# The delta rule's key and query lengths: squares in feature layout, summed by TensorE with a column of ones, in place of transposes and statistics

## The chip, the cores and the metric

The kernel runs on one core of one Trainium2 chip. The metric is the device time of one execution in microseconds (us). The engines are TensorE (PE, with its weight loads listed as PEld), VectorE (DVE), ScalarE (ACT), GpSimd (POOL) and the queue of SyncE (SP), which starts most loads of weights.

## The reference, cut to what matters

One inference step of a four-layer decoder: 256 new rows of a prompt (one sequence) and 8 single rows of samples, 1024 features. The mixers are pooling, gated delta rule, retention, pooling; each is followed by a SwiGLU block. The change is in the delta rule (layer 1), where queries and keys of each of 8 heads are divided by their lengths over 128 features:

```python
def l2norm(x):
    return x * lax.rsqrt(jnp.sum(x * x, -1, keepdims=True) + RMS_EPS)
...
    q = l2norm(qkv[..., :H * dk].reshape(B, T, H, dk)) * dk ** -0.5
    k = l2norm(qkv[..., H * dk:2 * H * dk].reshape(B, T, H, dk))
    v = qkv[..., 2 * H * dk:].reshape(B, T, H, dv)
    beta = jax.nn.sigmoid(b_logit)
    ...
    o, S = gated_delta_rule(q, k, v, g, beta, S0.astype(F32))
```

The delta rule then solves, for each head and chunk, a triangular system made of the products of keys with keys, and multiplies its result with values, queries and a running state.

## The kernel before, in words

All activations lie with features on the 128 partitions and the 264 rows (T: 256 prompt rows, then 8 sample rows) along the free axis. Weights come in chunks of 128 x 2048 and are split into a high and a low part (ScalarE casts at L205 and L231, VectorE or GpSimd subtracts at L206 and L232), so a projection is three fast matmuls for each block (`mm3`, all of them on L123, the line of the matmul helper; transposes are on L128).

The delta-rule layer (`gdn_layer`) takes heads in four pairs. It has 16 projections, two heads each, in the order of the list `jobs`: four of keys, one gate, then queries, values and gates mixed. After a projection come a short convolution (VectorE, L651 and L654) and SiLU (ScalarE, L657); the keys of all pairs stand in `kt` (128 x 8 x 264), queries in tiles of the tag `qv0`.

`lengths` gives the reciprocal lengths of one pair with rows on partitions, as `ssq` (128 x 2 heads x 3 columns: two chunks of 128 prompt rows and one of the 8 samples). Because lengths are sums over partitions in the feature layout, it transposes: four transposes of 128 x 128 into one PSUM tile `pk`, two of the sample columns into `pks`. For the heads in `onv` VectorE takes bn_stats and bn_aggr (mean and variance, from which the sum of squares is made); for the others ScalarE squares and sums (L802). GpSimd raises to the power -1/2 (L810, L811). `ON_V` says that both heads of key pairs 0 and 1, and the second head of pairs 2 and 3, go to VectorE; queries go to ScalarE.

Small PSUM tiles (`sm_ps`, tag `sm`) share four buffers; those of projections (`mm`) have four others. SBUF tiles of one tag share `bufs` buffers, one where none is given.

Most instructions are ordered by a scheduler that simulates the engines and starts what is ready, in the order of the program where there is a choice. From `PE.pinned = True` on, each TensorE instruction is kept behind the TensorE instruction written before it. There the work is woven by hand: `weave(main, fill, ratio)` runs one piece of `main` and then `ratio` steps of `fill` on average, a step being one block (`mm3`, three matmuls) of a projection; a piece ends at each `yield`. `turns` goes round several generators, `seq` runs them one after the other. Before that point the key lengths of pairs 0 to 2 are made, then the gate's projection, then the lengths of pair 3. The first woven part is `inverse` for all pairs (it begins with `br`, the key lengths times beta, on GpSimd at L819, then transposes of `br` and products of keys with keys, L825 and L831 on VectorE); the next are `operands`, `sample` and `outputs` for pairs 0 and 1, then for 2 and 3. The query lengths are the last thing in `operands`, after the products of keys with queries (L926); they are needed at the end of `outputs`.

Of the kernel before, what the change touches and what calls it, by code (L numbers as in the profile page):

```python
# [11 lines left out]
F32 = mybir.dt.float32  # L12
F32R = mybir.dt.float32r
BF16 = mybir.dt.bfloat16
AF = mybir.ActivationFunctionType
ALU = mybir.AluOpType
ADD, SUB, MUL, MAX, MIN, POW = ALU.add, ALU.subtract, ALU.mult, ALU.max, ALU.min, ALU.pow
AX = mybir.AxisListType

P = 128  # L20
TP = 256
NB = 8
T = TP + NB
# [6 lines left out]
RMS_EPS = 1e-6  # L30
DK = 128
# [9 lines left out]
RATIO = (0.8, 2, 1)  # L41

LO_FROM, LO_PARTS = 5, (0, 1, 3)
ON_V = ((0, 1), (0, 1), (1,), (1,))
ON_G = (3, 5, 7)
ATANH = (1.0000000039388743, 0.3333315796753999, 0.2001242686175498, 0.13980709417099926, 0.14087328632969365)

# [64 lines left out]
def body(ctx: ExitStack, tc: tile.TileContext, ap):  # L112
    nc = tc.nc
    V, S, G = nc.vector, nc.scalar, nc.gpsimd
# [29 lines left out]
    def C(name):  # L144
        o, n = CL[name]
        return cst[:, o:o + n]
# [5 lines left out]
    ident, U, sl, ones, o1024 = (C(n) for n in ("ident", "u", "sl", "ones", "o1024"))  # L152
    mhalf = pers.tile([P, 24], F32, name="mhalf")
# [34 lines left out]
    def nm(s):  # L188
        uid[0] += 1
        return f"{s}_{uid[0]}"  # L190
# [6 lines left out]
    def sm_ps(shape):  # L197
        return psm.tile(shape, F32, tag="sm", name=nm("sm"))
# [422 lines left out]
    def gdn_layer(l, pln):  # L621
        gp = ctx2.enter_context(tc.tile_pool(name="gdn", bufs=1))
# [36 lines left out]
        kt = gp.tile([P, H, T], F32, name="kt")  # L659
# [31 lines left out]
        for t in range(3):  # L691
            n = P if t < 2 else NB
# [76 lines left out]
        rks, rqs, brs, kgs, kbs, vbs, ats, tts, oss, oos = ({} for _ in range(10))  # L769

        def tile4(tag, bufs=1, dt=F32):
            return gp.tile([P, 2, 2, P], dt, tag=tag, name=nm(tag), bufs=bufs)

        def ct(tag, bufs=2):
            return gp.tile([P, 2, 3], F32, tag=tag, name=nm(tag), bufs=bufs)

        def hsl(a, p):
            return a[:, :, 2 * p:2 * p + 2].rearrange("p t h -> p h t")

        def lengths(src, tag, onv=()):  # L780

            pk, pks = sm_ps([P, 2, 2, P]), sm_ps([P, 2, P])
            ssq = ct(tag, 4)
            V.memset(ssq[:, :, 2], 1.0)
            if onv:
                mv = gp.tile([P, 2, 3, 2], F32, tag="mv", name=nm("mv"), bufs=2)
                V.memset(mv[:, :, 2], 1.0)
            for h in range(2):
                for c in range(2):
                    PE.transpose(pk[:, h, c], src[h][:, c * P:(c + 1) * P], ident)  # L790
            for h in range(2):
                PE.transpose(pks[:NB, h], src[h][:, TP:T], ident)
            for h in range(2):
                jk = gp.tile([P, P], F32, tag="junk", name=nm("junk"))
                for c in range(3):
                    n, a = (P, pk[:, h, c]) if c < 2 else (NB, pks[:NB, h])
                    if h in onv:
                        bs = gp.tile([P, 6], F32, tag="bs", name=nm("bs"), bufs=2)
                        V.bn_stats(bs[:n], a)
                        V.bn_aggr(mv[:n, h, c], bs[:n])  # L800
                    else:
                        S.activation(jk[:n], a, AF.Square, accum_out=ssq[:n, h, c:c + 1])  # L802
                if h in onv:
                    sh = ssq[:, h]
                    V.tensor_tensor(sh, mv[:, h, :, 0], mv[:, h, :, 0], MUL)
                    V.tensor_tensor(sh, sh, mv[:, h, :, 1], ADD)
                    V.tensor_scalar(sh, sh, float(DK), None, MUL)
            V.tensor_scalar(ssq, ssq, RMS_EPS, None, ADD)
            mh = mhalf[:, 0:6].rearrange("p (a b) -> p a b", a=2)
            G.tensor_tensor(ssq[:, :, 0:2], ssq[:, :, 0:2], mh[:, :, 0:2], POW)  # L810
            G.tensor_tensor(ssq[:NB, :, 2], ssq[:NB, :, 2], mh[:NB, :, 2], POW)  # L811
            return ssq

        def inverse(p):
# [84 lines left out]
        def operands(p):  # L899

            h0 = 2 * p
            q, v, rk, br = qt[p], vt[p], rks[p], brs[p]
            skg, skb = ct("skg"), ct("skb")
            G.tensor_tensor(skg[:, :, 0:2], rk[:, :, 0:2], hsl(egk, p)[:, :, 0:2], MUL)
            G.tensor_tensor(skb[:, :, 0:2], br[:, :, 0:2], hsl(egc, p)[:, :, 0:2], MUL)
            pk = sm_ps([P, 2, 2, P])
            for h, c in hc:
                PE.transpose(pk[:, h, c], kt[:, h0 + h, c * P:(c + 1) * P], ident)
            kg = kgs[p] = tile4("t1", 4)
            kb = kbs[p] = lnp.tile([P, 2, P], F32, tag="sq", name=nm("kb1"), bufs=2)  # L910
            V.tensor_tensor(kg, pk, skg[:, :, 0:2].unsqueeze(3).to_broadcast([P, 2, 2, P]), MUL)
            for h in range(2):
                S.mul(kb[:, h], pk[:, h, 1], skb[:, h, 1:2])
            yield
            pv = sm_ps([P, 2, 2, P])
            for h, c in hc:
                PE.transpose(pv[:, h, c], v[:, h, c * P:(c + 1) * P], ident)
            vb = vbs[p] = tile4("t1", 4)
            V.tensor_tensor(vb, pv, hsl(beta, p)[:, :, 0:2].unsqueeze(3).to_broadcast([P, 2, 2, P]), MUL)
            yield  # L920
            at = ats[p] = tile4("t2", 4)
            pqk = sm_ps([P, 2, 2, P])
            for h, c in hc:
                PE.matmul(pqk[:, h, c], kt[:, h0 + h, c * P:(c + 1) * P], q[:, h, c * P:(c + 1) * P], start=True, stop=True)
            for h, c in hc:
                V.scalar_tensor_tensor(at[:, h, c], pqk[:, h, c], rk[:, h, c:c + 1], dec[:, h0 + h, c], MUL, MUL)  # L926
            yield
            rqs[p] = lengths([q[:, h] for h in range(2)], "rq")

        def xz_tile(n):  # L930
            return pers.tile([P, 4, 4, P], F32, tag="xz", name=nm(n), bufs=2)
# [145 lines left out]
        def run(n):  # L1077
            for _ in range(n):
                kind, p = jobs.pop(0)
                yield from gate(p, next(ops)) if kind == 3 else proj(kind, p, kind == 1 and p < 3, next(ops))  # L1080

        def drain(g):
            for _ in g:
                pass

        for p in range(4):
            drain(run(1))
            if p < 2:
                for m in range(4 * p, 4 * p + 4):
                    pln.apply(m)  # L1090
        G.tensor_copy(ksg, kt[:, :, TP:T])
        for p in range(4):
            if p == 3:
                drain(run(JOBS[0]))
            rks[p] = lengths([kt[:, 2 * p + h] for h in range(2)], "rk", ON_V[p])
        PE.pinned = True
        weave(turns(*(inverse(p) for p in range(4))), run(JOBS[1]), RATIO[0])
        weave(seq(turns(operands(0), operands(1)), turns(sample(0), sample(1), outputs(0), outputs(1))), run(JOBS[2]), RATIO[1])
        weave(seq(turns(operands(2), operands(3), finish(0), finish(1)), turns(sample(2), sample(3), outputs(2), outputs(3))), run(len(jobs)), RATIO[2])
        PE.pinned = False  # L1100
        pss, raws = {}, {}
# [204 lines left out]
    for l in range(DEPTH):  # L1306
        with ExitStack() as ctx2:
            ln = (pool_layer, gdn_layer, ret_layer)[l % 3](l, *((l // 3, ln) if l % 3 == 0 else (ln,)))
        ln = ffn(l, ln)
# [94 lines left out]
```

## Time and profile before

| | |
|---|---|
| Time, three runs | median 1396.97 us (1396.32 to 1398.08) |
| The profiled execution | 1399.02 us |
| Its span, first to last instruction | 1397.2 us |
| TensorE, VectorE, ScalarE, GpSimd busy | 1326.9, 1044.3, 841.8, 460.2 us |
| Mean granted clock of TensorE | 0.978 of full speed |

The busy times are of one execution, and an engine that is busy for most of the span need not be so in each stretch of it; the granted clock is 1.0 at 2.4 GHz and 0.5 at 1.2 GHz. Matmuls are pipelined, so the durations of neighbours overlap: the step from one to the next is shorter than the duration of one.

### The profile page before, as it was taken

How to read it: one execution, taken by the hardware profiler on the slowest of the kernel's cores; microseconds unless marked ns; L12 is line 12 of the kernel's file. 1: busy time of each engine (PE TensorE's matmuls, PEld its weight loads, DVE VectorE, ACT ScalarE, POOL GpSimd, SP SyncE). 2: the span in 40 equal slices, each digit the busy share in tenths (PEclk: the TensorE clock that was granted, in tenths of full speed). 3: DMA queues.
4: the chain of work that ended last, by engine and by line, in shares of the span. 5: the costliest groups of instructions: out<-in, count | busy, mean ns of one | idle time of the engine just before them, and what ended most of it. 6: DMA issues, size and time to landing. Idle time of an engine off the chain costs nothing. (4 is left out here: it accounts for less than half of the span.)

```text
span 1397.2 us, 27688 instructions
## 1 busy us (share of the span) xinstructions
PE 1326.9 (95%) x10506; PEld 1273.5 (91%) x10509; DVE 1044.3 (75%) x2075; ACT 841.8 (60%) x1971; POOL 460.2 (33%) x518
## 2 busy tenths in 40 slices
PE   6999999879999999999979999999999998999996
PEld 4999999778998999999979999999998995999996
DVE  8885566989666799777697777668976758975564
ACT  4774544658564677675566665557765654774543
POOL 5230013563353443001278664133300144330022
PEclk8999999889999999999989999999999999999998
DMA  6355555421323355895645554456589961355550
GB/s 230 121 183 181 181 174 185 151 90 63 105 77 110 132 211 184 305 325 210 235 148 181 197 195 137 150 181 271 182 343 388 347 212 67 132 201 182 181 178 35
DMA packets 44341, 257.06 MB, mean 184 GB/s; under 512 B 5040, under 2 KB 9776, under 8 KB 16560
## 3 DMA queue, kind: packets, MB, share of 16 engines
q1 hardware_dynamic: 35936, 223.17, 44.9%
q10 hardware_dynamic: 5968, 19.55, 3.9%
q0 software_dynamic: 2304, 12.58, 2.2%
q8 instruction: 82, 1.34, 0.4%
q14 instruction: 51, 0.42, 0.1%
HBM read 238.45 MB, written 16.84 MB: 183 GB/s over the span
## 5 line engine op out<-in xcount | busy, mean ns | idle before, releaser
L206 DVE TENSOR_TENSOR l<-raw,h 128x512 fp32r<-128x512 f32 x658 | 463.1, 739 | 121.7 <-ACT h L205 116.9
L205 ACT CAST h<-raw 128x512 fp32r<-128x512 f32 x680 | 386.9, 616 | 193.9 <-PE mm L123 155.5
L123 PE MATMUL mm<-xh,h 128*128 128x264 f32 x1216 | 348.1, 288 | 8.2 <-ACT xh L394 4.0
L123 PE MATMUL mm<-xl,h 128*128 128x264 f32 x1216 | 348.4, 287 | 5.1 <-DVE xl L395 5.1
L123 PE MATMUL mm<-xh,l 128*128 128x264 f32 x1216 | 346.3, 287 | 0.0
L123 PEld LDWEIGHTS mm<-xh,h 128*128 128x128 f32 x1216 | 230.1, 190 | 10.8 <-ACT xh L394 4.8
L123 PEld LDWEIGHTS mm<-xl,h 128*128 128x128 f32 x1216 | 230.4, 189 | 5.9 <-DVE xl L395 5.3
L123 PEld LDWEIGHTS mm<-xh,l 128*128 128x128 f32 x1216 | 229.4, 189 | 0.7 <-DVE l L206 0.4
L123 PE MATMUL mm<-gh,l 128*128 128x264 f32 x704 | 199.6, 285 | 0.6 <-DVE l L206 0.6
L123 PE MATMUL mm<-gh,h 128*128 128x264 f32 x704 | 200.0, 284 | 0.0
L123 PE MATMUL mm<-gl,h 128*128 128x264 f32 x704 | 198.9, 283 | 0.0
L123 PE MATMUL mm<-zh,l 128*128 128x266 f32 x496 | 140.9, 289 | 3.0 <-DVE l L206 2.9
L123 PE MATMUL mm<-zh,h 128*128 128x266 f32 x496 | 142.1, 291 | 0.9 <-DVE ab L403 0.6
L123 PE MATMUL mm<-zl,h 128*128 128x266 f32 x496 | 142.5, 289 | 0.0
L123 PEld LDWEIGHTS mm<-gh,l 128*128 128x128 f32 x704 | 132.1, 188 | 1.0 <-DVE l L206 0.9
L123 PEld LDWEIGHTS mm<-gh,h 128*128 128x128 f32 x704 | 132.5, 188 | 0.1
L123 PEld LDWEIGHTS mm<-gl,h 128*128 128x128 f32 x704 | 132.5, 188 | 0.0
L404 POOL TENSOR_TENSOR ab<-ab,u 128x264 f32<-128x264 f32 x68 | 66.7, 992 | 138.5 <-DVE ab L403 59.6
L123 PE MATMUL mm<-xh,w 128*128 128x264 f32 x416 | 107.9, 314 | 2.1 <-DVE ab L403 2.1
L123 PEld LDWEIGHTS mm<-zh,l 128*128 128x128 f32 x496 | 92.9, 189 | 4.4 <-DVE l L206 4.1
L123 PEld LDWEIGHTS mm<-zh,h 128*128 128x128 f32 x496 | 93.1, 189 | 2.5 <-DVE ab L403 2.0
L123 PEld LDWEIGHTS mm<-zl,h 128*128 128x128 f32 x496 | 93.9, 189 | 1.0 <-DVE zl L300 0.2
(401 smaller groups left out, 2699.8 us busy)
## 6 DMA issues: line engine op xcount, KB each, us to landing
raw<-in_w_dram SPq DMA_DIRECT2D x132, 1024.0 KB
raw<-in_rwi_dram SPq DMA_DIRECT2D x24, 1024.0 KB
raw<-in_gwi_dram SPq DMA_DIRECT2D x16, 1024.0 KB
st<-in_rst_dram ACTq DMA_DIRECT2D x8, 1024.0 KB
raw<-in_rwo_dram SPq DMA_DIRECT2D x8, 1024.0 KB
st<-in_rst_dram SPq DMA_DIRECT2D x8, 1024.0 KB
vbc<-vdr SPq DMA_DIRECT2D x8, 1024.0 KB
out_ret_s_dram<-st POOLq DMA_DIRECT2D x8, 1024.0 KB, 10.6
```

Source lines behind the costliest of these rows:

```text
L123: i = nc.tensor.matmul(*a, **k)
L205: S.copy(hi[:, w], src_ap[:, w])
L206: (E or V).tensor_tensor(lo[:, w], src_ap[:, w], hi[:, w].bitcast(F32), SUB)
L404: (E or G).tensor_tensor(out, out, u[:n], ADD)
```

## The change

The squares are taken once for each pair, in the feature layout, by one ScalarE instruction over both heads and all 264 rows, into an SBUF tile of the new tag `lsq`. TensorE then sums over the partitions: six matmuls with a block of squares as the stationary operand and one column of ones as the moving one, each giving the sums of up to 128 rows as a column on partitions. VectorE adds the small constant while it reads PSUM, and GpSimd takes the power of all six columns at once. `lengths` becomes a generator with a `yield` between the Square and the matmuls; for keys it is drained at once, for queries the `yield` is one more place at which `weave` puts in projection steps. `ON_V` goes.

```diff
--- before.py
+++ after.py
@@ -41,7 +41,6 @@
 RATIO = (0.8, 2, 1)
 
 LO_FROM, LO_PARTS = 5, (0, 1, 3)
-ON_V = ((0, 1), (0, 1), (1,), (1,))
 ON_G = (3, 5, 7)
 ATANH = (1.0000000039388743, 0.3333315796753999, 0.2001242686175498, 0.13980709417099926, 0.14087328632969365)
 
@@ -777,38 +776,21 @@
         def hsl(a, p):
             return a[:, :, 2 * p:2 * p + 2].rearrange("p t h -> p h t")
 
-        def lengths(src, tag, onv=()):
-
-            pk, pks = sm_ps([P, 2, 2, P]), sm_ps([P, 2, P])
+        def lengths(src, tag):
+
+            sq = gp.tile([P, 2, T], F32, tag="lsq", name=nm("lsq"))
+            S.activation(sq, src, AF.Square)
+            yield
+            pq = sm_ps([P, 2, 3])
+            for h in range(2):
+                for c in range(3):
+                    n = P if c < 2 else NB
+                    PE.matmul(pq[:n, h, c:c + 1], sq[:, h, c * P:c * P + n], ones[:, 0:1], start=True, stop=True)
             ssq = ct(tag, 4)
             V.memset(ssq[:, :, 2], 1.0)
-            if onv:
-                mv = gp.tile([P, 2, 3, 2], F32, tag="mv", name=nm("mv"), bufs=2)
-                V.memset(mv[:, :, 2], 1.0)
-            for h in range(2):
-                for c in range(2):
-                    PE.transpose(pk[:, h, c], src[h][:, c * P:(c + 1) * P], ident)
-            for h in range(2):
-                PE.transpose(pks[:NB, h], src[h][:, TP:T], ident)
-            for h in range(2):
-                jk = gp.tile([P, P], F32, tag="junk", name=nm("junk"))
-                for c in range(3):
-                    n, a = (P, pk[:, h, c]) if c < 2 else (NB, pks[:NB, h])
-                    if h in onv:
-                        bs = gp.tile([P, 6], F32, tag="bs", name=nm("bs"), bufs=2)
-                        V.bn_stats(bs[:n], a)
-                        V.bn_aggr(mv[:n, h, c], bs[:n])
-                    else:
-                        S.activation(jk[:n], a, AF.Square, accum_out=ssq[:n, h, c:c + 1])
-                if h in onv:
-                    sh = ssq[:, h]
-                    V.tensor_tensor(sh, mv[:, h, :, 0], mv[:, h, :, 0], MUL)
-                    V.tensor_tensor(sh, sh, mv[:, h, :, 1], ADD)
-                    V.tensor_scalar(sh, sh, float(DK), None, MUL)
-            V.tensor_scalar(ssq, ssq, RMS_EPS, None, ADD)
-            mh = mhalf[:, 0:6].rearrange("p (a b) -> p a b", a=2)
-            G.tensor_tensor(ssq[:, :, 0:2], ssq[:, :, 0:2], mh[:, :, 0:2], POW)
-            G.tensor_tensor(ssq[:NB, :, 2], ssq[:NB, :, 2], mh[:NB, :, 2], POW)
+            V.tensor_scalar(ssq[:, :, 0:2], pq[:, :, 0:2], RMS_EPS, None, ADD)
+            V.tensor_scalar(ssq[:NB, :, 2], pq[:NB, :, 2], RMS_EPS, None, ADD)
+            G.tensor_tensor(ssq, ssq, mhalf[:, 0:6].rearrange("p (a b) -> p a b", a=2), POW)
             return ssq
 
         def inverse(p):
@@ -925,7 +907,7 @@
             for h, c in hc:
                 V.scalar_tensor_tensor(at[:, h, c], pqk[:, h, c], rk[:, h, c:c + 1], dec[:, h0 + h, c], MUL, MUL)
             yield
-            rqs[p] = lengths([q[:, h] for h in range(2)], "rq")
+            rqs[p] = yield from lengths(q, "rq")
 
         def xz_tile(n):
             return pers.tile([P, 4, 4, P], F32, tag="xz", name=nm(n), bufs=2)
@@ -1083,6 +1065,9 @@
             for _ in g:
                 pass
 
+        def key_lengths(p):
+            rks[p] = yield from lengths(kt[:, 2 * p:2 * p + 2], "rk")
+
         for p in range(4):
             drain(run(1))
             if p < 2:
@@ -1092,7 +1077,7 @@
         for p in range(4):
             if p == 3:
                 drain(run(JOBS[0]))
-            rks[p] = lengths([kt[:, 2 * p + h] for h in range(2)], "rk", ON_V[p])
+            drain(key_lengths(p))
         PE.pinned = True
         weave(turns(*(inverse(p) for p in range(4))), run(JOBS[1]), RATIO[0])
         weave(seq(turns(operands(0), operands(1)), turns(sample(0), sample(1), outputs(0), outputs(1))), run(JOBS[2]), RATIO[1])
```

## Rows read from the trace of the kernel before

**Rows 1.** The page, busy time of engines.

```profile
PE 1326.9 (95%) x10506; PEld 1273.5 (91%) x10509; DVE 1044.3 (75%) x2075; ACT 841.8 (60%) x1971; POOL 460.2 (33%) x518
```

**Rows 2.** Stretches: us; busy PE, PEld, DVE, ACT, POOL; clock; DMA share; GB/s.

```profile
286.00:288.00 2.00, 0.60 (x5) 0.39 (x4) 1.75 (x8) 2.00 (x9) 1.19 (x1) 1.00 0.00 0
288.00:290.00 2.00, 1.35 (x6) 0.96 (x6) 2.00 (x11) 1.80 (x6) 1.51 (x4) 0.63 0.47 74
...
302.00:304.00 2.00, 2.00 (x19) 2.00 (x19) 2.00 (x5) 0.00 (x0) 1.09 (x1) 0.96 0.00 0
```

**Rows 3.** Timeline of TensorE, 284.5 to 298.3: start, us, line, tiles, [idle before <- releaser].

```profile
286.32 0.28 PE L123 MATMUL mm<-xh,w 128*128 128x264 f32 x1
288.65 1.51 PE L128 MATMUL sm<-cst,kt 128*128 128x128 f32 x6 [2.05 <-DVE bs L799]
292.84 1.51 PE L128 MATMUL sm<-cst,kt 128*128 128x128 f32 x6 [2.68 <-DVE bs L799]
294.00 0.57 PE L123 MATMUL mm<-xh,w 128*128 128x264 f32 x1
...
295.91 0.42 PE L123 MATMUL mm<-xh,w 128*128 128x264 f32 x1
297.22 1.12 PE L128 MATMUL sm<-cst,br 128*128 128x128 f32 x4 [0.88 <-POOL br L819]
```

**Rows 4.** Tile `bs`: durations in ns (least/median/most), first and last start.

```profile
L799 DVE BATCH_NORM_STATS2 bs<-sm x18: 269/286/301, 286.9 to 295.5; 128x6 f32<-128x128 f32 x12, 8x6 f32<-8x128 f32 x6
L800 DVE BATCH_NORM_AGGREGATE mv<-bs x18: 136/162/182, 287.3 to 295.9; 128x2 f32<-128x6 f32 x12, 8x2 f32<-8x6 f32 x6
```

**Rows 5.** Busy time, the stretch of operands, samples and outputs.

```profile
376.00:470.00 94.00, 89.95 (x739) 83.74 (x738) 60.87 (x169) 52.54 (x192) 40.21 (x63) 1.00 0.30 102
```

**Rows 6.** Timeline of TensorE, 378 to 388 and 429 to 440.

```profile
382.13 1.47 PE L128 MATMUL sm<-cst,qv 128*128 128x128 f32 x12
384.78 0.38 PE L128 MATMUL sm<-cst,qv 128*8 128x128 f32 x2 [1.18 <-ACT junk L802]
385.17 0.24 PE L123 MATMUL sm<-cst,qp 128*8 128x1 f32 x4
...
435.61 0.60 PE L128 MATMUL sm<-cst,qv 128*8 128x128 f32 x4 [1.15 <-DVE t L926]
```

**Rows 7.** Timeline of GpSimd, 292 to 298.

```profile
292.42 1.05 POOL L810 TENSOR_TENSOR rk<-rk,mhalf 128x4 f32<-128x4 f32 x1 [1.19 <-DVE mv L800]
293.46 0.70 POOL L811 TENSOR_TENSOR rk<-rk,mhalf 8x2 f32<-8x2 f32 x1
...
296.97 0.20 POOL L819 TENSOR_TENSOR br<-rk,rc 128x4 f32<-128x4 f32 x1
```

**Rows 8.** Groups of ScalarE by shape, 280 to 500: busy us, mean ns | idle before.

```profile
L1030 ACT ACTIVATE junk<-t 128x128 f32<-128x128 f32 x16 | 5.0, 311 | 0.7 <-DVE t L1018 0.4
...
L302 ACT ACTIVATE sq<-d 128x264 f32<-128x264 f32 x8 | 3.2, 413 | 1.1 <-POOL s L318 1.1
```

**Rows 9.** Timeline of TensorE, 303 to 306.

```profile
304.77 1.06 PE L123 MATMUL sm<-kt 128*128 128x128 f32 x8
```

**Rows 10.** Tile `qp`: durations in ns (least/median/most), first and last start.

```profile
L123 PE MATMUL sm<-cst,qp x16: 163/163/171, 385.2 to 437.2; 128*8 128x1 f32 x16
```

**Rows 11.** Groups of TensorE by shape, 265 to 274: busy us, mean ns | idle before.

```profile
L123 PE MATMUL sm<-g,cst 128*128 128x8 f32 x8 | 1.9, 364 | 1.9 <-POOL g L727 1.9
```

**Rows 12.** Timeline of ScalarE, 283 to 296.

```profile
283.16 2.55 ACT L657 ACTIVATE kt<-kt,zb 128x264 f32<-128x264 f32 x6
...
287.27 0.53 ACT L657 ACTIVATE kt<-kt,zb 128x264 f32<-128x264 f32 x1
...
289.07 0.49 ACT L1071 ACTIVATE sz<-mm,zb 128x264 f32<-128x264 f32 x1
```

**Rows 13.** Timeline of VectorE, 298 to 302.

```profile
298.37 0.69 DVE L825 TENSOR_TENSOR t<-dec,sm 128x512 f32<-128x512 f32 x1 [1.20 <-PE sm L128]
300.08 1.13 DVE L831 SCALAR_TENSOR_TENSOR t<-sm,rk,t 128x128 f32<-128x128 f32 x4 [1.02 <-PE sm L123]
```

## The prediction, made before the result was known

> **What bounds the kernel now.** I read the page first: TensorE is busy for 95% of the span [rows 1], so in most of the kernel only two things change the time: TensorE's own work, and holes in it. Then I listed busy time in stretches of 2 us through the delta-rule layer. The key lengths show there as a hole: from 286 to 288 TensorE works 0.60 of 2 us while VectorE is full [rows 2]. From the clock means of two stretches its fall and return follow: 0.63 in 288 to 290 is 0.52 us at full speed (2.4 GHz) and the rest at half (1.2 GHz), so it fell at about 288.52; 0.96 in 302 to 304 gives the return at about 302.16 [rows 2]. Before the fall TensorE had lacked work since 286.6; before the return it had worked unbroken from 297.22 [rows 3].
>
> The order of TensorE's work tells why [rows 3]. The transposes of pair 2 wait 2.05 us and those of pair 3 wait 2.68 us, both for VectorE's statistics (L799): each pair holds two of the four small PSUM buffers until its statistics have read them. Everything after is written down as pinned behind these transposes, so the next projection starts at 294.00, and the first transposes of the inverse (`br`) at 297.22 after 0.88 us of waiting for GpSimd. The statistics themselves are 18 BATCH_NORM_STATS2 of 0.286 and 18 aggregates of 0.162 us, 8.1 us on VectorE [rows 4]. So this stretch is bound by VectorE, and that is the work the change removes.
>
> In the query part TensorE is busy 89.95 of 94 us at full clock [rows 5]: there every microsecond of TensorE work counts, and of the holes two belong to this code, 1.18 us behind ScalarE's squares (L802) and 1.15 us behind L926, both before transposes of the eight sample columns [rows 6].
>
> **The change, part by part.** *VectorE.* The 8.1 us go, with the small products behind them; two additions of 1e-6 per pair come. This is only worth what the new chain is shorter.
>
> *GpSimd.* Two powers, 1.05 and 0.70 us [rows 7], become one over six columns: 1.05 plus twice the step per column, (1.05-0.70)/2, about 1.4 us. `br` of pair 0 is then ready by about 291 (Square 286.3, matmuls 287.4, sums 287.7, power begun when GpSimd's cast is done, at most 2.5 us later), before TensorE can use it; the 0.88 us wait goes.
>
> *ScalarE.* One Square of 528 columns for each pair. The nearest rows are 0.413 us for 264 columns and 0.311 for 128 [rows 8]: 0.00075 us a column, so 0.413+0.198=0.61 us; bounds 0.413 and 0.83. For keys of pair 2 and 3 and for all queries it replaces squares that TensorE had to wait for.
>
> *TensorE.* Per pair six transposes go, 0.11 us each (two last 0.38 us and twelve 1.47, so ten more steps 1.09 [rows 6]; one alone lasts 0.27), 0.65 us. Six fp32 matmuls come, and an fp32 matmul is two instructions: the four `kt` products are eight [rows 9]. Twelve instructions, then: eight load 128 weight columns, four load 8, and all move one column. The trace has 8-column loads with one moving column: four in 0.24 us, of which the last takes 0.163 [rows 6, 10], 0.026 each. For 128-column loads with few moving columns it has one row, at half clock: eight in 1.9 us with a mean of 0.364 for one, (1.9-0.364)/7=0.22 each [rows 11]. At full clock I take 0.11, half of it, which is also the step of the `kt` products, (1.06-0.27)/7. A pair costs 8x0.11+4x0.026=0.98 us at full clock and 1.9 at half; bounds 0.31 (all at 0.026) and 1.9.
>
> By the Trainium skill, "TensorE: Matmul & The Clock Gate", section "LDWEIGHTS (loading the stationary operand)", a load takes its columns divided by 1.2 per ns: 107 ns for 128, and the formula has no clock in it. By that an estimated 0.98 us would hold at half clock too; the row at half clock speaks against it, and the sum goes by the row.
>
> *The wait that is added.* The tile of squares has one buffer. Square 1 waits until the matmuls of pair 0 have read it, and so on: a chain ScalarE, TensorE, ScalarE. On ScalarE what is queued behind a Square are weight casts and the evacuation `sz`; on TensorE, the pinned projection and the inverse.
>
> *The keys, step by step.* The six activations of pairs 0 to 2 leave ScalarE at 285.7 [rows 12]; Square 0 runs from there to 286.3. TensorE has finished the gate by then (twelve transposes are out of its way, 1.3 us). Matmuls 0 to 287.25. ScalarE is busy with pair 3's activations until 287.8 [rows 12], so Square 1 ends at 288.45: the clock has fallen or falls now, as TensorE has done less since 285 than it did before. At half clock a step is 0.05 (hand-over: `br` ends at 297.17, TensorE begins at 297.22 [rows 3, 7]) + 1.9 + 0.2 + 0.05 + 0.61 = 2.8 us. Matmuls 1 end at 290.4, 2 at 293.2, 3 at 296.0. The projection's nine matmuls took 2.3 us at half clock [rows 3], about 2.0 of issue; `br` of pair 0 begins at about 298.0, against 297.22: 0.8 us late. But TensorE then works unbroken from about 294, where it had a hole until 297.22. So I let the clock return as much earlier, 3.2 us: at 298.9. From 297.22 to 302.16 TensorE did 4.94 us at half, worth 2.47 at full; now 0.9 us at half (0.45) and 2.02 at full end it at 300.9, 1.2 us sooner. VectorE's 0.69+1.13 us per pair [rows 13] can keep up for that much. Term: -1.2 us. If the clock returns at 302.16 as before: +0.4.
>
> *The queries.* The new yield puts Square 0 and Square 1 a turn ahead, but both sets of matmuls come one right after the other in TensorE's pinned order, since the generators end there. So: 0.98, then 0.163+0.05+0.61+0.05=0.87 us of waiting for Square 1, then 0.98: 2.83 us, and two transposes 0.22, 3.05. Before, from 382.13 to 385.17, 3.04 us [rows 6]. The second two pairs have the same form and a like wait (1.15). Term: 0, bounds -2 (fewer-column loads at 0.026) and +1.2 (each Square held by one more instruction on ScalarE). Extra yields pull six projection steps forward; their number is fixed, so nothing is added.
>
> *Sum.* -1.2 us. The profiled execution took 1399.02 us, 1.8 of it around its span of 1397.2; it is 2.05 us (0.15%) above the median of the runs, 1396.97. From the median: **1395.8 us**, a change of -0.09%. No change is what can't be told from 0.2%, or 2.8 us.
>
> **The rivals.** *Full clock.* The few-column matmuls keep the clock up. A step is then 0.61+0.05+0.98+0.163+0.05=1.85 us, the chain ends near 293, the projection's nine matmuls at 0.12 by 294.3, and `br` begins 2.9 us earlier and at full clock. The 2.47 us end at 296.8, not 302.16: 5.4 us; VectorE, beginning about 3.4 us earlier and full from then on, allows less. I take 4.5: **1392.5**. For it: TensorE's share of the chain is half. Against: in 286 to 288 it did 0.60 of 2 us and the clock fell.
>
> *ScalarE holds the Squares (slower).* ScalarE works in order, and from 285.7 to 289.56 it has 3.85 us of other work [rows 12]. If all of it falls into hand-overs instead of beside TensorE's matmuls, the chain grows by 3.85; with one more instruction before each query Square, 1.2. Together **1400.9** (1395.8+5.05). It decides from 4.0 us in all. Against: it needs every gap to be hit, and half the chain leaves ScalarE free.
>
> *Loads at 0.11 at either clock.* Three pairs shrink by 8x(0.22-0.11)=0.88 us each, 2.6 in all: **1393.2**. The row at half clock is against it [rows 11]. The rule of the page named above gives this case.
>
> **How the numbers follow.** Chances: forecast 0.52, full clock 0.26, ScalarE 0.14, loads 0.08. Faster: 0.24 of the second, 0.06 of the fourth, 0.03 from the forecast's own edge, 0.33. Slower: 0.11 of the third and 0.03, 0.14. Same: 0.53. The forecast's own range is 1394 to 1399.5 (the two clock returns, the query bounds, one or two held Squares). The full-clock case with the query gain of 2 us ends at 1390.5, the ScalarE case near 1400.5 short of its worst: these are my range.
>
> **What would show it.** Right: no BATCH_NORM on these lines, four Squares between 285.6 and 294 about 2.8 us apart, clock at half for several of them, `br` of pair 0 without a wait at 297 to 298.5, the clock's return near 299, and one wait of about 0.9 us in each query part. Wrong: Squares 1.9 us apart with the clock at full, `br` at 294; or Squares late behind casts; or a 128-column load with one moving column that takes far from 0.11 us; or a shift that begins outside these stretches.

## The result, and the profile after

The changed kernel takes 1413.8 us (median; 1413.0 to 1414.61) against 1396.64 (1396.03 to 1398.08) for the kernel before: ratio 1.0119, 95% interval 1.0106 to 1.0132. It is 17.2 us slower, where 1395.8 was forecast and the range ended at 1400.5. Its profiled execution took 1414.07 us with a span of 1412.2, 15.0 us more than the span of before; the mean granted clock is 0.971 (0.978 before).

Where the 15.0 us came in is read by setting the same instruction of both traces side by side (lines of the new kernel are one to eighteen lower; starts in us):

| First start of | before | after | difference |
|---|---|---|---|
| SiLU of the keys | 283.16 | 284.39 | 1.2 |
| `br` transposes | 297.22 | 302.20 | 5.0 |
| matmul `sm<-identb,tx` in the inverse | 310.98 | 317.56 | 6.6 |
| `kt` transposes of `operands`(0) | 374.20 | 380.92 | 6.7 |
| `kt` transposes of `operands`(2) | 421.04 | 431.17 | 10.1 |
| ScalarE's first cast `gh<-s` in the layer's SwiGLU | 511.63 | 529.75 | 18.1 |
| the end | 1397.24 | 1412.22 | 15.0 |

The first 1.2 us lie ahead of the changed code. Then 3.8 us come in the key lengths, 1.6 in the inverse behind them, 3.4 around the first query lengths and 8.0 around the second. About 3 are given back far away: the records of before have half clock near 1162 and 1173 us, those of after have none there.

The page's line of busy times says little, as TensorE is busy for 95% in both [rows 1]: of the added 13.4 us of TensorE much is the same work at half clock.

```profile
PE 1340.3 (95%) x10557; PEld 1287.3 (91%) x10557; DVE 1036.1 (73%) x2025; ACT 835.4 (59%) x1919; POOL 459.0 (33%) x510
```

TensorE's timeline of after, 286 to 318, answers to [rows 3]; then ScalarE's, 284 to 300, to [rows 12]:

```profile
286.21 0.29 PE L122 MATMUL mm<-xh,w 128*128 128x264 f32 x1
287.53 1.39 PE L122 MATMUL sm<-cst,lsq 128*128 128x1 f32 x12 [1.03 <-ACT lsq L782]
291.92 2.21 PE L122 MATMUL sm<-cst,lsq 128*128 128x1 f32 x12 [2.99 <-ACT lsq L782]
294.92 2.21 PE L122 MATMUL sm<-cst,lsq 128*128 128x1 f32 x12 [0.79 <-ACT lsq L782]
297.92 2.21 PE L122 MATMUL sm<-cst,lsq 128*128 128x1 f32 x12 [0.79 <-ACT lsq L782]
300.06 0.59 PE L122 MATMUL mm<-xh,w 128*128 128x264 f32 x1
...
302.20 1.06 PE L127 MATMUL sm<-cst,br 128*128 128x128 f32 x4
...
315.94 0.61 PE L122 MATMUL sm<-identb,lm 128*128 128x128 bf16 x4 [3.79 <-DVE lm L836]
```

```profile
284.39 2.55 ACT L656 ACTIVATE kt<-kt,zb 128x264 f32<-128x264 f32 x6
286.85 0.63 ACT L782 ACTIVATE lsq<-kt 128x528 f32<-128x528 f32 x1
287.38 1.13 ACT L230 CAST w<-raw 128x512 fp32r<-128x512 f32 x2
...
289.81 1.14 ACT L230 CAST w<-raw 128x512 fp32r<-128x512 f32 x2
290.84 0.49 ACT L1053 ACTIVATE sz<-mm,zb 128x264 f32<-128x264 f32 x1
291.21 0.65 ACT L782 ACTIVATE lsq<-kt 128x528 f32<-128x528 f32 x1
294.22 0.64 ACT L782 ACTIVATE lsq<-kt 128x528 f32<-128x528 f32 x1 [2.36 <-PE sm L122]
```

The chain is there: Square, twelve instructions, Square, 3.00 us from one to the next (294.22 to 297.22). But the second Square starts at 291.21, behind four casts, pair 3's activations and both `sz`, and TensorE stands for 2.99 us.

The clock, by stretches of after (columns as in [rows 2]: the granted clock is the third number from the end):

```profile
288.00:290.00 2.00, 0.92 (x10) 0.77 (x9) 0.91 (x3) 2.00 (x9) 1.42 (x2) 1.00 0.03 8
290.00:292.00 2.00, 0.08 (x1) 0.09 (x1) 0.18 (x1) 1.86 (x4) 2.00 (x3) 0.63 0.61 119
302.00:304.00 2.00, 2.00 (x11) 2.00 (x11) 0.69 (x1) 0.00 (x0) 0.06 (x1) 0.50 0.00 0
304.00:306.00 2.00, 2.00 (x19) 2.00 (x19) 1.31 (x5) 0.14 (x1) 0.00 (x0) 0.95 0.00 0
314.00:316.00 2.00, 0.06 (x1) 0.07 (x2) 2.00 (x4) 0.00 (x0) 1.60 (x2) 0.61 0.66 193
...
392.00:396.00 4.00, 3.67 (x23) 3.13 (x24) 0.92 (x6) 1.36 (x4) 4.00 (x4) 0.62 0.10 39
396.00:400.00 4.00, 4.00 (x24) 3.46 (x23) 2.29 (x8) 0.36 (x1) 0.50 (x3) 0.53 0.00 0
436.00:440.00 4.00, 2.21 (x9) 1.86 (x10) 2.60 (x7) 1.07 (x5) 0.66 (x3) 0.66 0.90 342
440.00:444.00 4.00, 4.00 (x19) 3.65 (x18) 2.22 (x4) 0.14 (x1) 0.00 (x0) 0.50 0.00 0
448.00:452.00 4.00, 3.21 (x27) 2.99 (x26) 1.21 (x6) 0.64 (x1) 1.55 (x2) 0.87 0.75 262
```

The old fall moves from 288.5 to 290.5. Four falls of 6.8 us each are new, at 314.4, 392.9, 437.3 and 451.0; the kernel before ran this stretch at full clock (1.00 in 304 to 376 and in 376 to 470 [rows 5]). The first comes while TensorE stands for 3.79 us, the third while it stands for 3.83 us; the second and fourth come at the second set of query sums:

```profile
390.31 1.29 PE L122 MATMUL sm<-cst,lsq 128*128 128x1 f32 x12
392.33 1.80 PE L122 MATMUL sm<-cst,lsq 128*128 128x1 f32 x12 [0.73 <-ACT lsq L782]
...
437.79 0.69 PE L127 MATMUL sm<-cst,t 128*128 128x128 f32 x2 [3.83 <-DVE t L1022]
...
448.30 1.28 PE L122 MATMUL sm<-cst,lsq 128*128 128x1 f32 x12
450.38 1.80 PE L122 MATMUL sm<-cst,lsq 128*128 128x1 f32 x12 [0.79 <-ACT lsq L782]
```

The wait of 3.83 us is in the end of `outputs`(1), not in a query length. GpSimd's timeline of after, 428 to 440, shows what goes on there: the power L1019, which the scaling of the outputs needs, is followed by two weight subtractions before L1020 goes on.

```profile
432.11 1.36 POOL L1019 TENSOR_TENSOR rr<-ms,mhalf 128x6 f32<-128x6 f32 x1
433.42 2.51 POOL L231 TENSOR_TENSOR w<-raw,w 128x512 fp32r<-128x512 f32 x2
435.89 0.39 POOL L1020 TENSOR_TENSOR rr<-rr,rq 128x6 f32<-128x6 f32 x1
```

### The profile page after: what moved, and what is told of

Read it like the earlier page. It is cut to its first block, busy times and chain, and to the rows that moved or that the text cites. A ratio compares the mean times of both kernels' runs of the same rounds, so it can differ in the third digit from the quotient of the medians.

```text
span 1412.2 us, 27671 instructions
## 1 busy us (share of the span) xinstructions
PE 1340.3 (95%) x10557; PEld 1287.3 (91%) x10557; DVE 1036.1 (73%) x2025; ACT 835.4 (59%) x1919; POOL 459.0 (33%) x510
## 5 line engine op out<-in xcount | busy, mean ns | idle before, releaser
L122 PE MATMUL mm<-gh,h 128*128 128x264 f32 x704 | 200.1, 284 | 0.0
L122 PE MATMUL mm<-xh,w 128*128 128x264 f32 x416 | 113.1, 326 | 2.1 <-DVE ab L402 2.1
```

The source lines that it names most:

```text
L122: i = nc.tensor.matmul(*a, **k)
```

## The experiments

The theory formed from these rows has three parts: (1) keys, a serial chain on one buffer, late through ScalarE's queue, and a longer wait in the inverse; (2) queries, 24 one-column matmuls nearly in a row, at which the clock falls; (3) the extra `yield`, which takes projection steps from in front of the wait at 437.79. Rivals: the keys alone, the queries alone, or the plain cost of matmuls and Squares without the clock.

So that parts can be told apart, each profile is cut into three: A from the first key SiLU to the first matmul `identb,tx`, B from there to ScalarE's first cast `gh<-s` of the layer's SwiGLU, C to the last instruction. Each row comes from the starts of these instructions in one trace; the falls in B are the lengths of the stretches at half clock that lie between 320 and 500 us.

| Kernel | A, us | B, us | C, us | falls in B, us |
|---|---|---|---|---|
| before | 27.8 | 200.6 | 885.6 | none |
| after | 33.2 | 212.2 | 882.5 | 6.8, 6.8, 6.8 |
| e2, new keys | 32.9 | 200.6 | 885.6 | none |
| e3, new queries | 27.8 | 210.5 | 883.4 | 3.4, 6.8, 6.8 |
| e4, no query yield | 33.2 | 206.1 | 882.5 | 3.4, 6.8 |
| e5, 64 columns | 32.0 | 208.6 | 885.8 | 3.4, 6.8 |
| e1, two buffers | 30.2 | 208.7 | 883.0 | 6.8, 3.4, 3.4 |
| e8, VectorE squares | 29.9 | 211.9 | 885.4 | 3.4, 6.8, 6.8 |
| e7, spread | 30.3 | 203.1 | 882.1 | 6.8 |
| e9, old keys, spread | 25.6 | 200.6 | 884.7 | none |
| e10, side by side | 25.6 | 205.8 | 887.8 | 3.4, 6.8 |
| e11, the same, 64 columns | 26.8 | 201.9 | 885.6 | none |
| e12, mixed keys | 29.0 | 200.1 | 883.1 | none |

**e2, the keys' part alone** (`lengths_old` is `lengths` of the kernel before).

```diff
-            rqs[p] = yield from lengths(q, "rq")
+            rqs[p] = lengths_old([q[:, h] for h in range(2)], "rq")
```

> Keys as after, queries as before. Theory 1 (the changed kernel loses at three separate places: the serial chain of the key lengths, the clock that falls behind the few-column matmuls of the queries, and a wait of finish that the moved projection steps uncover): only the first is left, about 5 us slower than before (3.75 us until br, 1.6 us in the inverse), the clock at full from 330 to 500. Rival (one rescheduling of the whole layer, no matter which part is changed): more than 10 us slower still.

Measured: 1405.73 us against 1397.42, ratio 1.0066 (1.0043 to 1.0089). **e3, the queries' part alone:**

```diff
-            drain(key_lengths(p))
+            rks[p] = lengths_old([kt[:, 2 * p + h] for h in range(2)], "rk", ON_V[p])
```

> Queries as after, keys as before. Theory 1: about 11 us slower than before (two clock falls of 3.4 us each at the query lengths, 3.8 us of waiting in finish with another clock fall behind it), the stretch up to the inverse as before. Rival (one rescheduling): as the changed kernel, 15 us slower or more, or nothing.

Measured: 1406.25 us, ratio 1.0061 (1.0041 to 1.0080). The two medians add up: 8.3 + 8.8 = 17.1 us of the 17.2. That they do so this closely is partly luck, as e2 was expected about 5 us slower and its five runs go from 1404.17 to 1412.65 (its profile, the fastest, has a span 5.2 us above that of before). The table shows the places: e2 has 5.1 of the 5.4 us of A and none of B, e3 none of A and 9.9 of the 11.6 us of B, with a first fall of 3.4 us in place of 6.8. TensorE's waits, first of e2, then of e3, 280 to 480 (total us, times, longest), show each with its own wait of 3.8 us:

```profile
PE sm L122 <- ACT lsq L782: 5.9, 4, 3.0
PE sm L122 <- DVE lm L870: 3.8, 1, 3.8
```

```profile
PE sm L128 <- DVE t L1057: 3.8, 1, 3.8
```

**e4, no yield for queries** (keys as in after).

```diff
             S.activation(sq, src, AF.Square)
-            yield
+            if tag == "rk":
+                yield
```

> As after, but no yield between Square and matmuls of the queries, so no projection steps are moved. Theory 1: the 3.8 us wait before the transposes of finish and the clock fall behind it go, some 7 us faster than after; the two clock falls at the query lengths stay, and TensorE's wait for the first Square grows. Rival (the finish wait comes from elsewhere, for instance from GpSimd's order): the wait stays, within 2 us of after.

Measured: 1407.83 us, ratio 1.0076 (1.0061 to 1.0091), about 6 us less than after. The wait of 3.83 us is gone: in TensorE's waits of e4 the end of `outputs` has only the 1.0 us for `os` that before had too. The fall of 437 is gone with it, the two at the query sums stay (the first is half as long). The wait for the Squares was expected to grow and did not: it is 7.1 us in after too. The two weight subtractions stand behind the power here as well (3.00 us), and nothing waits for them. What differs is when the power begins: 4.2 us ahead of the `kt` transposes of `operands`(2) in e4 (424.60 and 428.76), as in before (4.1 us), but 0.9 us behind them in after (432.11 and 431.17).

```profile
PE sm L122 <- ACT lsq L782: 7.1, 6, 3.0
...
PE sm L127 <- DVE os L1024: 1.0, 1, 1.0
```

**e5, 64 columns of ones** (the first of the 64 equal sums is read).

```diff
-            pq = sm_ps([P, 2, 3])
+            pq = sm_ps([P, 2, 3, 64])
...
-                    PE.matmul(pq[:n, h, c:c + 1], sq[:, h, c * P:c * P + n], ones[:, 0:1], start=True, stop=True)
+                    PE.matmul(pq[:n, h, c], sq[:, h, c * P:c * P + n], ones[:, 0:64], start=True, stop=True)
```

> As after, but each of the matmuls with ones moves 64 columns instead of one (only the first is read). Theory 1 (the clock falls because these matmuls move few columns): TensorE takes about the same time for them, the clock stays at full behind the query lengths, some 6.8 us faster than after. Rival (the clock falls because of the 0.8 us wait for the second Square): the falls stay, same time as after or a little slower.

Measured: 1411.26 us, ratio 1.0096 (1.0075 to 1.0117). That is 2.5 us less than after, where 6.8 were expected. Of the falls in B the last is gone and the first is half as long; the wait of 3.84 us and its fall stay. In the keys, where the clock is low anyhow, the wider matmuls lengthen the step, from 3.00 to 3.59 us; A is 1.2 us shorter all the same, as the wait for `lm` is 2.1 us instead of 3.8 and no fall comes there. TensorE's timeline of e5:

```profile
294.65 2.79 PE L122 MATMUL sm<-cst,lsq 128*128 128x64 f32 x12 [0.79 <-ACT lsq L782]
298.24 2.79 PE L122 MATMUL sm<-cst,lsq 128*128 128x64 f32 x12 [0.79 <-ACT lsq L782]
```

**e1, two buffers for the squares** (`gdg` takes a tag of another tile, for the space).

```diff
-            sq = gp.tile([P, 2, T], F32, tag="lsq", name=nm("lsq"))
+            sq = gp.tile([P, 2, T], F32, tag="lsq", name=nm("lsq"), bufs=2)
```

> As after, with two buffers for the squares (a small tile gives up its own space for it). Theory 1a (the serial chain on one buffer sets the end of the key lengths): Squares 1 and 2 no longer wait for the matmuls before them, the last matmuls of the key lengths end some 4 us earlier, about where the transposes of before ended, and the 0.8 us waits in the queries go; 5 to 8 us faster than after, the finish wait stays. Rival (half clock and 128-column loads set the length, not the buffer): the key lengths end within 1.5 us of after.

Measured: 1408.25 us against 1397.49, ratio 1.0083 (1.0065 to 1.0102). The chain is cut: `br` comes 14.5 us after the first key SiLU (17.8 in after, 14.1 in before). Yet A is still 2.4 us longer than before's, as the wait of 3.8 us for `lm` stays. TensorE's timeline of e1:

```profile
289.14 1.39 PE L122 MATMUL sm<-cst,lsq 128*128 128x1 f32 x12 [0.70 <-ACT lsq L782]
291.97 4.34 PE L122 MATMUL sm<-cst,lsq 128*128 128x1 f32 x24 [1.44 <-ACT lsq L782]
```

More than half of the gain is in B. There no Square is waited for any more, and the sums of both pairs stand in one row:

```profile
387.35 2.61 PE L122 MATMUL sm<-cst,lsq 128*128 128x1 f32 x24
```

The clock falls behind both rows all the same (at 390.0 and 448.0, with TensorE busy). The wait for the Square is thus not what makes it fall.

**e8, the keys' squares on VectorE.**

```diff
-            S.activation(sq, src, AF.Square)
+            if tag == "rk":
+                V.tensor_tensor(sq, src, src, MUL)
+            else:
+                S.activation(sq, src, AF.Square)
```

> As after, but the squares of the keys are products on VectorE, one buffer still. Theory 1b (ScalarE's queue held Square 1 for about 2 us behind casts, pair 3's activations and an evacuation): the matmuls of pair 1 begin about 2 us earlier, and so does the end of the key lengths. Rival (the chain's length is the matmuls' alone): under 0.7 us.

Measured: 1413.94 us, ratio 1.0121 (1.0102 to 1.0141): no gain. A is 3.3 us shorter than after's. Counted from the first SiLU, the sums of pair 1 begin 1.9 us earlier (5.6 us, 7.5 in after) and the last sums end 1.4 us earlier (14.4, 15.7), since VectorE's squares are waited for as well; so ScalarE's queue cost about that much. The rest comes behind it, where the fall is 3.4 us instead of 6.8. In this profile C is 2.9 us longer, with a fall of 6.8 us at 1176.2 that the profile of after lacks. Whether that holds in the timed executions can't be seen.

**e7, spread** (two buffers; the Square before the products of keys with queries, its sums right behind them, as many yields as before).

```diff
+            lq = lengths(q, "rq")
+            next(lq)
             pqk = sm_ps([P, 2, 2, P])
...
+            rqs[p] = yield from lq
             yield
-            rqs[p] = yield from lengths(q, "rq")
```

> Two buffers, and in the queries the Square ahead of the products of keys with queries and the matmuls with ones right behind them, with projection steps between the two pairs and as many yields as before. Theory 1 (three separate losses): no clock fall at the query lengths, no 3.8 us wait in finish, key lengths as with two buffers; 12 to 16 us faster than after, within 4 us of before. Rival (few-column matmuls let the clock fall wherever they stand): the falls stay, at least 7 us slower than before.

Measured: 1400.16 us, ratio 1.0023 (1.0012 to 1.0035): 13.6 us less than after. The wait at the end of `outputs` is gone; the 3.8 us for `lm` in the keys stay, as in e1. Of the three falls in B one is left, though none was expected, and it comes at the second of two spread sets, with no wait ahead. TensorE's timeline of e7 and the clock there:

```profile
434.68 1.29 PE L122 MATMUL sm<-cst,lsq 128*128 128x1 f32 x12
437.26 1.39 PE L122 MATMUL sm<-cst,lsq 128*128 128x1 f32 x12
```

```profile
438.00:440.00 2.00, 2.00 (x12) 1.45 (x13) 2.00 (x11) 0.00 (x0) 1.44 (x1) 0.55 0.87 266
```

So the rival, that such matmuls let the clock fall wherever they stand, is not ruled out by e7.

**e9, old keys with the spread queries** (e7 with the edit of e3; two small tiles share a buffer, for the space).

> Keys as before (transposes and statistics), queries as in the spread version. Theory 1: the two waits of 1.2 us that the old query lengths had go, some 1.3 us of TensorE work comes, no clock falls: within 2 us of before, if anything faster. Rival (few-column matmuls let the clock fall wherever they stand): 3 to 7 us slower.

Measured: 1394.64 us, ratio 0.9985 (0.9973 to 0.9996), the only kernel below the one before. The table says that this is not the queries' doing: B is 200.6 us, as before. A is 2.2 us shorter, with `br` as long after the first SiLU as before, but the clock is back 13.9 us after that SiLU (298.1 to 284.2) instead of 19.0. So query lengths by squares and ones cost nothing and gain nothing when they are spread and the clock stays up; in e7, with the same order, it fell once, and B is 203.1 us. **e10, side by side** (e9, but the Square behind the products of keys with queries and the sums of both pairs next to each other, with as many yields; the edit is shown against after), and **e11**, e10 with the 64 columns of e5:

```diff
             pqk = sm_ps([P, 2, 2, P])
...
+            lq = lengths(q, "rq")
+            next(lq)
             yield
-            rqs[p] = yield from lengths(q, "rq")
+            rqs[p] = yield from lq
```

> As the version with old keys and spread queries, but the matmuls with ones of the two pairs stand side by side in TensorE's order, with two buffers and as many yields. Theory 1c (24 few-column instructions in a row let the clock fall, without any wait): one fall at each of the two places, 2 to 6 us slower than the spread version. Rival (it was the 0.8 us wait and the single buffer): no fall, within 1 us of the spread version.

> As the side-by-side version, moving 64 columns of ones instead of one. Theory 1c: the same instructions with more columns let the clock stay, or fall for a shorter time; 1 to 4 us faster than side by side with one column. Rival (the number of moved columns is of no account): same time or slower by the longer instructions.

Measured against 1396.33: e10 1402.91 us, ratio 1.0046 (1.0030 to 1.0063); e11 1398.75, ratio 1.0012 (1.0003 to 1.0022). TensorE's timelines of e9, e10 and e11 have no wait ahead of any of these rows:

```profile
379.78 1.29 PE L123 MATMUL sm<-cst,lsq 128*128 128x1 f32 x12
381.83 1.05 PE L123 MATMUL sm<-qv,kt 128*128 128x128 f32 x8
382.72 1.29 PE L123 MATMUL sm<-cst,lsq 128*128 128x1 f32 x12
```

```profile
381.19 2.61 PE L123 MATMUL sm<-cst,lsq 128*128 128x1 f32 x24
```

```profile
382.75 3.15 PE L123 MATMUL sm<-cst,lsq 128*128 128x64 f32 x24
```

The clock behind them, in e10 and then in e11, two stretches each:

```profile
384.00:386.00 2.00, 2.00 (x17) 1.43 (x16) 0.20 (x2) 0.36 (x1) 1.77 (x4) 0.67 0.35 147
386.00:388.00 2.00, 2.00 (x13) 1.97 (x12) 0.50 (x3) 1.21 (x3) 0.00 (x0) 0.50 0.00 0
```

```profile
384.00:386.00 2.00, 2.00 (x17) 1.42 (x16) 0.28 (x3) 0.00 (x0) 1.32 (x1) 1.00 0.95 397
386.00:388.00 2.00, 2.00 (x21) 1.56 (x20) 0.45 (x4) 0.72 (x2) 1.64 (x3) 1.00 0.13 53
```

TensorE is busy for all of the 2 us in every row, and in e10 it falls to half clock. Its falls of 3.4 and 6.8 us lose half of 10.2, 5.1 us; B is 5.1 us longer than e9's (205.77 against 200.63). The clock is known from one profile of each kernel. The times agree with it: the four runs of e10 go from 1400.00 to 1405.82 us, the ten of e11 from 1396.69 to 1400.25.

Set side by side, the profiles have this, a fall being one that begins during the sums of a place or at most 2.0 us behind them:

| Sums of two pairs at one place | kernels | places | followed by a fall |
|---|---|---|---|
| one column, next to each other | after, e3, e4, e8, e1, e10 | 12 | 12 |
| one column, with wide matmuls between | e7, e9, e12 | 6 | 1 |
| 64 columns, next to each other | e5, e11 | 4 | 1 |

In the first row e1 and e10 have no wait between the two sets, the other four kernels one of 0.7 to 0.8 us for the Square. So both spreading and more columns made the fall rarer here, and neither rules it out. Why one place of six falls (e7) and another with the same order does not (e9) is open.

**e12, mixed keys** (e9, with key pairs 2 and 3 by Square and ones, pairs 0 and 1 by transposes and statistics).

```diff
-            rks[p] = lengths_old([kt[:, 2 * p + h] for h in range(2)], "rk", ON_V[p])
+            if p < 2:
+                rks[p] = lengths_old([kt[:, 2 * p + h] for h in range(2)], "rk", ON_V[p])
+            else:
+                drain(key_lengths(p))
```

> As the version with old keys and spread queries, but key pairs 2 and 3 take the Square and the ones; pairs 0 and 1 keep transposes and statistics. Theory 2 (the hole of before comes from pairs 2 and 3 waiting for the small PSUM buffers and for VectorE): the transposes of br begin at about 293 to 295 instead of 297, 2 to 5 us faster than with old keys throughout. Rival (the inverse is bound by VectorE and its order, so an earlier start is lost again): within 1.5 us.

Measured: 1397.96 us, ratio 1.0007 (0.9998 to 1.0016): the same as before, and some 3 us slower than e9 (0.9985), where 2 to 5 us faster was expected; A is 29.0 us against 25.6. The two waits for statistics become one, and the place of the other is taken by a wait for `br`. GpSimd works without a gap from 290.98 to 299.37, and both powers of pairs 2 and 3 (L796) go ahead of the first `br`, which comes 15.0 us after the first SiLU instead of 13.8. TensorE's timeline of e12, then GpSimd's:

```profile
289.82 3.26 PE L123 MATMUL sm<-cst,lsq 128*128 128x1 f32 x24 [1.67 <-DVE bs L818]
299.61 1.12 PE L128 MATMUL sm<-cst,br 128*128 128x128 f32 x4 [4.26 <-POOL br L838]
```

```profile
293.43 1.37 POOL L796 TENSOR_TENSOR rk<-rk,mhalf 128x6 f32<-128x6 f32 x1
...
296.43 1.31 POOL L796 TENSOR_TENSOR rk<-rk,mhalf 128x6 f32<-128x6 f32 x1
```

## Why the prediction was wrong

**Prices that held.** The Square lasts 0.63 to 0.65 us (0.61 predicted). The power over six columns lasts 1.32 to 1.37 (1.4). Inside a set a 128-column load with one moving column steps by 0.11 us at full clock and 0.21 at half (0.11 and 0.22). So "Loads at 0.11 at either clock" is out, and with it the rule that the prediction cited from the Trainium skill, "TensorE: Matmul & The Clock Gate", section "LDWEIGHTS (loading the stationary operand)": its 107 ns agrees with the trace at full clock alone, and the measurement decides. A pair, though, costs 2.61-1.29=1.32 us at full clock and 4.34-2.21=2.13 at half, not 0.98 and 1.9. The prediction priced loads of 128 and of 8 columns as if each ran among its own kind; they alternate here.

**The keys, term -1.2 us: wrong in three steps.** A is 5.4 us longer (33.2 against 27.8). With the 1.2 us of the later start taken off:

| Step | predicted | measured |
|---|---|---|
| Square 1 ends | 288.45 | 290.63 |
| Squares 2 to 3 | 2.8 | 3.00 |
| `br` begins | 298.0 | 300.97 |
| clock back | 298.9 | 302.96 |

The step that failed first is "ScalarE is busy with pair 3's activations until 287.8 [rows 12], so Square 1 ends at 288.45": casts and both `sz` also went ahead of it, 2.2 us. This is the mechanism of "ScalarE holds the Squares", at one hand-over of several and with 2.2 of its 3.85 us. Second, "TensorE then works unbroken from about 294": it still stood for 0.79 us ahead of each of the last two sets, and the clock came back later than in before (302.16). Third, "VectorE's 0.69+1.13 us per pair [rows 13] can keep up for that much" fails: TensorE waits 3.79 us for `lm`, against 1.3 in before, and the clock falls again. e1 shows this apart from the chain, as `br` is nearly in time there and 2.4 us are lost all the same. That an earlier clock is worth about what the prediction hoped (half of the time gained at half clock) is borne out by e9: 5.1 us earlier, A 2.2 us shorter.

**The queries, term 0: the larger miss.** B is 11.6 us longer (212.2 against 200.6). Two sentences failed. "Extra yields pull six projection steps forward; their number is fixed, so nothing is added": the number was fixed, but the steps had covered the wait for the output scaling, and without them TensorE stood for 3.83 us; e4 and e7 remove the yield, and the wait goes. And the sum itself (0.98 + 0.87 + 0.98) took the full clock of [rows 5] as given for the new work. From the first set to the end of the second it took 3.82 us (390.31 to 394.13) instead of 2.83, with a wait of 0.73 instead of 0.87; what cost more came with it and behind it, in the 6.8 us at half clock. The prediction let the clock fall only where TensorE lacks work, and in e1 and e10 it fell with none lacking.

**The cases.** None of the four had a clock fall in the query part, so the range ended just short of the worst of the ScalarE case. Both signs of the keys' term were weighed, and neither could reach +17.

## What to carry to other kernels

Matmuls that move one column are short on paper and keep TensorE busy in the profile, but two sets in a row were followed by half clock here, and the work behind them pays: keep them apart with wide matmuls (a fall at 1 place of 6 in e7, e9 and e12) or give them more moving columns (1 of 4 in e5 and e11), against 12 of 12 otherwise. Steps of filler work that are moved are not free although their number stays: find the wait that each was covering. And where one buffer ties three engines into a chain, look at what is queued on each engine ahead of each hand-over, not only at the durations in the chain.

## What the runs showed of the hardware

- The clock went to half with TensorE busy for the whole stretch: 24 one-column matmuls in 2.61 us, then 0.67 and 0.50 granted (e10); with 64 columns, in 3.15 us, it stayed at 1.00 (e11); with eight products of 128 columns and projection matmuls between two sets of twelve it stayed too in e9 (B without a fall), but fell once in e7 (0.55 in 438 to 440).
- The same key code was at half clock for 13.7 us in before and e3 (A 27.8 us), 10.2 in e11 (26.8) and 6.8 in e9 and e10 (25.6). What decides between them is open, and so is why the falls in layer 3 come in some profiles (before, e8) and not in others (after): C varies from 882.1 to 887.8 us. The lead of e9 over the kernel before is no larger than this.
